# A gated ConvFFN in two stages, its up projection by seven half-size products per pair of column blocks (Strassen's algorithm)

## The chip, the cores and the metric

The kernel runs on one core of one Trainium2 chip. The metric is the device time of one execution in microseconds, as the median of the runs. Engines are named as the profile names them: PE is TensorE's matmul, PEld its weight load, DVE is VectorE, ACT is ScalarE, POOL is GpSimd and SP is the sync engine, whose queue issues most of the DMA transfers.

## The reference

Two trunk layers of a diffusion backbone are computed for 1024 latent tokens and 128 context tokens, 1152 tokens of width 1024 together. Layer 0 mixes with an S5 state-space branch and differential attention, layer 1 with a short convolution and an RG-LRU. Each mixer is followed by a ConvFFN, and every sub-layer stands between two RMSNorms with adaLN modulation. All is float32. The part that matters here:

```python
def conv_ffn(h, w_up, cw, cb, w_down):        # h (1152, 1024), w_up (1024, 5632), w_down (2816, 1024)
    u = dwconv(h @ w_up, cw, 1) + cb          # three taps over the tokens, each sequence by itself
    g, val = jnp.split(u, 2, axis=-1)         # 2816 columns of gate, 2816 of value
    return (jax.nn.gelu(g) * val) @ w_down

def _post(x, y, m, g, j):                     # x + gate * norm(y)
    return x + m[:, 3 * j + 2, None] * rmsnorm(y, g)
```

The modulation m is SiLU(cond) times a matrix of 1024 x 6144 for each layer.

## The kernel before

Matmuls take a rounded float32 type. To keep float32's accuracy each operand is held as two parts, `hi` (a rounded copy, made by ACT) and `lo` (the rest, a subtraction on DVE or POOL), and each product is three matmuls: hi hi, hi lo, lo hi (`mm3`, lines 81 to 87).

The order of the program is: setup and the first norm, S5 with its tables, attention, then `phase_c`: output projection (`mixer_out`), FFN of layer 0 (`ffn`, `down`, `ffn_end`), layer 1's mixer (`mixer1`), its output projection, and the FFN of layer 1. The instructions are written in this order, and a planner (the tile framework) fixes before the run in which order each engine gets them, by a simulated timeline, the order of the program as priority and the free buffers of the pools. On the chip each engine takes its instructions in that order and waits on semaphores.

`mixer_out` (one step for each of 9 token tiles of 128) ends in `pre`, which norms a tile, transposes it on PE, modulates it on ACT, and splits it into `hh` (DVE, line 289) and `hl` (POOL, line 290), the FFN's input as 8 blocks of 128 rows by 1152 tokens.

`ffn` runs over 22 pairs of a gate block and a value block of 128 columns. For each it loads two weight blocks of 512 KB (`wcol`), splits each on ACT (line 97) and DVE (line 99), and for three chunks of 386, 386 and 384 tokens computes both blocks, 24 matmuls each into one PSUM bank (`pps`). ACT scales the middle tap out of PSUM (line 1371), DVE adds the two outer taps, which read the product in PSUM and the sum in SBUF (line 1374), ACT takes the gelu, DVE multiplies gate by value (line 1392), and the result is split into `mh` and `ml` (lines 1393, 1394). Every second pair `down` multiplies the two newest finished pairs by their 128 rows of `w_down`, 9 tiles by 2 halves by 6 matmuls of 512 columns (`dps`), and DVE adds each half to `acc` (line 1420). The `lo` part of `w_down` is made on POOL (line 99). Beside the FFN of layer 0 run 28 pieces of the modulation (`mod_piece`, two per pair at first): 8 loads of 128 KB, 16 DVE instructions on 128x256 (lines 229, 231), a split and four matmuls each. `ffn_end` then does the post norm and the residual tile by tile, and in layer 0 the next pre norm.

`mixer1` makes 20 blocks of 128 columns by `proj`, three chunks of 384 tokens each; its gates are small matmuls of the same chunk width. `tap` (line 1482) is a convolution tap from SBUF to SBUF.

Of the kernel before, what the change touches and what calls it, by code (L numbers as in the profile page):

```python
# [9 lines left out]
F32 = mybir.dt.float32  # L10
# [7 lines left out]
T = 1152  # L18
TS = 1024
# [5 lines left out]
CHF = ((0, 386, 0, 385), (384, 770, 385, 769), (768, 1152, 769, 1152))  # L25


def f(ap):
    return ap.bitcast(F32)

# [23 lines left out]
class K:  # L54
# [59 lines left out]
    # ---------------------------------------------------------------- setup  # L114
    def setup(self):
# [13 lines left out]
        # selector stationaries: column v of ones  # L129
# [17 lines left out]
    # ------------------------------------------------------------ modulation  # L147
# [14 lines left out]
    def finish_row(self, ps, l, j, h0, w, rowp, tag, col=None):  # L162
        """rows of the modulation: + b, and the combination with the norm's gain"""
# [25 lines left out]
    def mod_pe(self, l, js, psp, rowp, tag, cols=None):  # L189
        """rows js of the modulation; a generator, one step for each piece of the weights"""  # L190
# [15 lines left out]
    def mod_cols(self, l, js, pool, ptag, psp, tag, bufs):  # L206
        """rows js of the modulation as columns [128, v, block]"""
# [54 lines left out]
    def post(self, x, y, tmp, ga):  # L262
        """x += gate * norm(y), y in parts"""
        nc = self.nc
        w = D // len(y)
        rs = self.rstd(self.sumsq(y, tmp if self.junk is None else self.junk), D)
        for i, p in enumerate(y):
            sl = slice(i * w, i * w + w)
            nc.vector.tensor_tensor(tmp[:, sl], p, ga[:, sl], op=OP.mult)
        nc.vector.scalar_tensor_tensor(x, tmp, rs, x, op0=OP.mult, op1=OP.add)  # L270

    def pre(self, t, x, tmp, cols, hh, hl):
        """norm of token tile t, transposed, modulated and split into hh, hl"""
# [4 lines left out]
        ts = slice(t * 128, t * 128 + 128)  # L278
        for q in range(2):
            ps = self.pt.tile([128, 4, 128], F32, tag="pt", name=self.nm("tps"))  # L280
            h = self.cv.tile([128, 4, 128], F32, tag="cv", name=self.nm("h"))
# [3 lines left out]
            for i in range(4):  # L285
                b = q * 4 + i
                nc.scalar.activation(h[:, i], ps[:, i], AF.Identity, scale=sc[:, b:b + 1], bias=sh[:, b:b + 1])
            hv = hh[:, q * 4:q * 4 + 4, ts]
            nc.vector.tensor_copy(hv, h)
            nc.gpsimd.tensor_tensor(hl[:, q * 4:q * 4 + 4, ts], h, f(hv), op=OP.subtract)  # L290
# [4 lines left out]
    # ------------------------------------------------------------- projections  # L295
# [46 lines left out]
    def expm1(self, x, one=0.0):  # L342
        """exp(x) - 1 (+ one) of a small array to float32's accuracy"""
# [34 lines left out]
    def unit(self, r, i):  # L378
        """bring a complex number's modulus back to 1"""
# [5 lines left out]
    # ------------------------------------------------------------ S5 parameters  # L385
    def s5_params(self, psp):
# [24 lines left out]
        # angle into [-pi, pi]  # L411
# [24 lines left out]
        # powers a^0 .. a^8  # L436
# [9 lines left out]
        # 10 powers for the read-out side: a^i (forward), a^(9-i) (backward)  # L446
# [5 lines left out]
        # phases e^(i phi) of a^8, and its doublings  # L452
# [7 lines left out]
        # write side: a^(7-j) (forward), a^j (backward), turned back by one chunk  # L460
# [19 lines left out]
        # initial states [ri, d, g, n] -> columns  # L480
# [6 lines left out]
        # first states, the backward scan's turned; one step of the recurrence on them  # L487
# [864 lines left out]
    def ffn(self, l, hh, hl, acc, back):  # L1352
# [4 lines left out]
        for fb in range(NFB):  # L1357
# [46 lines left out]
            if back:  # L1404
                self.mod_piece(*back.pop(0))
# [280 lines left out]
```

## Time and profile before

| what | before |
|---|---|
| median of 3 runs | 3000.33 us (2998.35 to 3001.52) |
| span of the profiled execution, first to last instruction | 2997.2 us |
| busy PE / PEld / DVE / ACT / POOL | 94% / 85% / 68% / 37% / 27% of the span |
| granted TensorE clock, mean | 0.974 of 2.4 GHz |

The profiled execution has no time of its own beside its span; the median of the runs is 3.1 us above it, which is what lies around the span. A busy share says how long an engine had an instruction in hand; an instruction that waits for something while it is in hand counts as busy. Matmuls are pipelined, so one matmul's duration is longer than the distance to the next one; the pace of a stream is its length over its count. In the views by stretch, the columns are the stretch, its length, the busy time and instruction count of PE, PEld, DVE, ACT and POOL, the granted clock, the DMA engines' busy share and GB/s.

### The profile page before, as it was taken

The page shows a single profiled execution, that of the slowest core. Times are in us where ns is not written, and L with a number is a line of the kernel's source. Part 1 is how long each engine was busy: PE and PEld are TensorE (multiplying, and loading weights), DVE is VectorE, ACT ScalarE, POOL GpSimd, SP SyncE. Part 2 cuts the span into 40 slices and gives each one's busy share as a digit, 9 for nine tenths or more (in the row PEclk, how much of TensorE's full clock was granted, in tenths as well). Part 3 has the DMA queues.
Part 4 walks back from the last instruction along what each step waited for, and adds up shares of the span by engine and source line. Part 5 has one row for each costly group of instructions (what it writes and reads, how often), then busy time and mean ns, then how long its engine had stood idle before and what let it go on. Part 6 is the DMA issues. An engine that isn't in the chain of part 4 may idle for free.

```text
span 2997.2 us, 40584 instructions
## 1 busy us (share of the span) xinstructions
PE 2816.8 (94%) x15196; PEld 2557.3 (85%) x15196; DVE 2035.9 (68%) x3572; ACT 1096.7 (37%) x1921; POOL 813.7 (27%) x982
## 2 busy tenths in 40 slices
PE   7976788888999999999999989999999999999998
PEld 3874566777789999999999979997899999999997
DVE  6777765988668888888655685455455555555557
ACT  5222113766454222322222365554532222222222
POOL 2699972877131000000000151112300000000001
PEclk9998899999999999999999999999999999999999
DMA  6434447552642333323211131124411111111113
GB/s 222 142 86 107 117 138 200 137 116 75 193 146 89 98 99 96 97 91 93 62 43 57 64 122 55 53 88 146 138 46 43 43 43 43 43 43 43 43 36 134
DMA packets 298835, 279.45 MB, mean 93 GB/s; under 512 B 45454, under 2 KB 259682, under 8 KB 298638
## 3 DMA queue, kind: packets, MB, share of 16 engines
q1 hardware_dynamic: 266168, 238.51, 25.8%
q0 software_dynamic: 14912, 23.21, 3.1%
q10 hardware_dynamic: 17558, 15.14, 1.8%
q8 instruction: 119, 1.95, 0.3%
q14 instruction: 78, 0.64, 0.1%
HBM read 220.59 MB, written 56.20 MB: 92 GB/s over the span
## 4 chain that ended last, share of the span: by engine, by line
PE 69%; DVE 6%; ACT 3%; issue 2%; DMA 1%; POOL 1%; ACTq 0%; DVEq 0%; POOLq 0%; SPq 0%
PE pps L87 43%; PE dps L87 16%; PE ops L87 6%; DVE e L1077 1%; DVE nb L1060 1%; PE sA L1055 1%; ACT e L1066 1%; PE gps L87 1%; PE tps L284 1%; DVE wh L1102 0%; DVE s L1114 0%; PE ops L1145 0%; DMA mw<-w_mod 0%; POOL hl L290 0%; PE gps L759 0%
## 5 line engine op out<-in xcount | busy, mean ns | idle before, releaser
L87 PE MATMUL pps<-hh,whi 128*128 128x384 f32 (+1 forms) x2880 | 977.0, 339 | 1.1 <-ACT whi L97 0.7
L87 PE MATMUL pps<-hh,wlo 128*128 128x384 f32 (+1 forms) x2880 | 974.7, 339 | 2.2 <-DVE wlo L99 2.2
L87 PE MATMUL pps<-hl,whi 128*128 128x384 f32 (+1 forms) x2880 | 974.7, 339 | 0.6 <-POOL hl L798 0.4
L87 PEld LDWEIGHTS pps<-hh,whi 128*128 128x128 f32 x2880 | 546.1, 190 | 17.5 <-issue 3.2
L87 PEld LDWEIGHTS pps<-hh,wlo 128*128 128x128 f32 x2880 | 545.6, 189 | 15.2 <-DVE wlo L99 3.2
L87 PEld LDWEIGHTS pps<-hl,whi 128*128 128x128 f32 x2880 | 546.4, 190 | 8.1 <-DVE hl L798 0.7
L99 POOL TENSOR_TENSOR wlo<-wr,whi 128x1024 fp32r<-128x1024 f32 x44 | 109.2, 2487 | 1455.3 <-PE dps L87 1162.5
L1374 DVE SCALAR_TENSOR_TENSOR cc<-pps,cvc,cc 128x255 f32<-128x255 f32 (+1 forms) x704 | 342.0, 511 | 145.0 <-ACT cc L1371 139.8
L1420 DVE TENSOR_TENSOR acc<-acc,dps 128x512 f32<-128x512 f32 x360 | 245.9, 683 | 232.5 <-PE dps L87 231.5
L1371 ACT ACTIVATE cc<-pps,cvc 128x383 f32<-128x383 f32 (+2 forms) x264 | 175.0, 665 | 414.1 <-PE pps L87 393.3
L87 PE MATMUL dps<-whi,mh 128*128 128x512 f32 x792 | 311.8, 394 | 1.2 <-DVE acc L1420 1.2
L87 PE MATMUL dps<-whi,ml 128*128 128x512 f32 x792 | 312.0, 394 | 0.0
L87 PE MATMUL dps<-wlo,mh 128*128 128x512 f32 x792 | 310.5, 392 | 0.0
L97 ACT ACTIVATE whi<-wr 128x1024 fp32r<-128x1024 f32 x168 | 177.7, 1059 | 278.3 <-PE pps L87 196.6
L99 DVE TENSOR_TENSOR wlo<-wr,whi 128x1024 fp32r<-128x1024 f32 x124 | 153.9, 1243 | 85.4 <-PE pps L87 70.4
L231 DVE SCALAR_TENSOR_TENSOR macc<-mw,sil,macc 128x256 f32<-128x256 f32 x392 | 174.9, 482 | 18.9 <-DMA mw<-w_mod 18.1
L87 PEld LDWEIGHTS dps<-whi,ml 128*128 128x128 f32 x792 | 148.8, 188 | 33.7
L87 PEld LDWEIGHTS dps<-whi,mh 128*128 128x128 f32 x792 | 149.2, 188 | 20.8 <-DVE acc L1420 2.4
L87 PEld LDWEIGHTS dps<-wlo,mh 128*128 128x128 f32 x792 | 149.2, 188 | 18.8
L1389 ACT ACTIVATE cc<-cc 128x385 f32<-128x385 f32 x132 | 69.3, 525 | 248.1 <-DVE cc L1374 232.2
L1104 POOL TENSOR_TENSOR wl<-wf,wh 128x512 fp32r<-128x512 f32 (+2 forms) x96 | 144.4, 1523 | 52.5 <-DVE ra L1074 44.1
L1394 DVE TENSOR_TENSOR ml<-cc,mh 128x385 fp32r<-128x385 f32 x132 | 118.2, 899 | 34.2 <-ACT mh L1393 34.2
(356 smaller groups left out, 4171.6 us busy)
## 6 DMA issues: line engine op xcount, KB each, us to landing
wr<-ffn_w_up SPq DMA_DIRECT2D x88, 512.0 KB
mw<-w_mod SPq DMA_DIRECT2D x224, 128.0 KB
x<-x SPq DMA_DIRECT2D x45, 512.0 KB
wr<-ffn_w_down SPq DMA_DIRECT2D x44, 512.0 KB
wm<-w_mod SPq DMA_DIRECT2D x40, 512.0 KB
k<-kh POOLq DMA_DIRECT2D x8, 1408.0 KB, 6.4
wr<-w_in_cd SPq DMA_DIRECT2D x20, 512.0 KB
yr<-y SPq DMA_DIRECT2D x17, 512.0 KB
```

Source lines behind the costliest of these rows:

```text
L87: nc.tensor.matmul(ps, x, y, start=first and i == 0 and j == 0, stop=last and i == n - 1 and j == 2)
L97: nc.scalar.activation(hi, raw, AF.Copy)
L99: (eng or nc.vector).tensor_tensor(lo, raw, f(hi), op=OP.subtract)
L231: nc.vector.scalar_tensor_tensor(acc[v], wt, s, acc[v], op0=OP.mult, op1=OP.add)
L284: nc.tensor.transpose(ps[:, i], tmp[:, b * 128:(b + 1) * 128], self.id)
L1055: pin(nc.tensor.matmul(A[:, c:c + w], heads[u.h, 2][:, m, u.q0:u.q0 + 128], heads[u.h, m][:, j, u.k0 + c:u.k0 + c + w], start=j == 0, stop ...
L1104: pin((nc.vector if late else nc.gpsimd).tensor_tensor(vl, u.wf[b][:, :k], f(vh), op=OP.subtract))
L1371: nc.scalar.activation(cc[:, :no], ps[:, q:q + no], AF.Identity, bias=cw[3], scale=cw[1])
L1374: nc.vector.scalar_tensor_tensor(cc[:, oa - o0:ob - o0], ps[:, oa + d - i0:ob + d - i0], cw[j], cc[:, oa - o0:ob - o0], op0=OP.mult, op1=O ...
L1389: nc.scalar.activation(cc[:, :no], cc[:, :no], AF.Gelu_apprx_tanh)
L1394: nc.vector.tensor_tensor(ml[:, o0:o1], g[1][:, :no], f(mh[:, o0:o1]), op=OP.subtract)
L1420: nc.vector.tensor_tensor(acc[t][:, sl], acc[t][:, sl], ps, op=OP.add)
```

## The change

The FFN becomes two stages. `up` writes the rows gelu(g) * val of each pair to DRAM (`m`, 576 KB a pair, by SP); `down` reads them back by token tiles in three groups of 8, 8 and 6 pairs, splits them there, and sums a group's products in two PSUM banks before one addition to `acc`. In the third group each tile's post norm (`ffn_fin`) follows its sum at once.

In `up`, gate and value block form a 2x2 matrix A (rows: gate, value; columns: lower and upper 512 of the inner dimension) and the input a 2x2 matrix B (inner halves by token halves of 576). `forms` builds four combinations T1 to T4 of B's blocks once per layer; `block` builds four combinations of A's blocks per pair on POOL, splits seven half-size weights (four `lo` parts on DVE, three on POOL), makes seven products of 24 matmuls of 288 columns, and adds them up. The convolution then reads the finished rows from SBUF. One piece of the modulation follows each pair in layer 0; the other six go with `down`. The mixer's projections work in two halves of 576 tokens, 48 matmuls of 288 columns each, and PSUM is three double banks and two single ones. The pools become `big` (14 buffers of 9 KB per partition), `mid` (8) and `wr` (8 of 4 KB).

```diff
+    def pair(self, raw, eng, pool=None):
+        p = (pool or self.wr).tile([128, 2] + shape[1:], F32R, tag="big" if pool else "wr", ...)
+        self.nc.scalar.activation(p[:, 0], raw, AF.Copy)
+        eng.tensor_tensor(p[:, 1], raw, f(p[:, 0]), op=OP.subtract)
+    def prod(self, prs, ys, name):
+        ps = self.bank2(name)
+        steps = [(p[:, x, k], y[j][:, k]) for p, y in zip(prs, ys) for k in range(4) for x, j in ((0, 0), (0, 1), (1, 0))]
+        for n, (x, y) in enumerate(steps):
+            for c in range(2):
+                nc.tensor.matmul(ps[:, c, :w], x, y[:, c * w:c * w + w], ...)
+    def forms(self, H):
+        def whole(out, q, n, k, eng):
+            eng.tensor_tensor(out, f(h[:, k]), f(l[:, k]), op=OP.add)
+        def put(i, k, src, eng):
+            nc.scalar.activation(h[:, k], src, AF.Copy)
+            eng.tensor_tensor(l[:, k], src, f(h[:, k]), op=OP.subtract)
+        for k in range(4):
+            whole(A[:, 0], 0, 0, k, G)
+            whole(A[:, 1], 1, 1, k, V)
+            V.tensor_tensor(A[:, 0], r12, A[:, 0], op=OP.subtract)
+            V.tensor_tensor(B[:, 0], A[:, 1], A[:, 0], op=OP.subtract)
+            put(1, k, B[:, 0], G)
+            put(0, k, A[:, 0], V)
+            whole(B[:, 1], 1, 0, k, G)
+            V.tensor_tensor(A[:, 1], A[:, 1], r12, op=OP.subtract)
+            put(2, k, A[:, 1], G)
+            V.tensor_tensor(B[:, 1], B[:, 0], B[:, 1], op=OP.subtract)
+            put(3, k, B[:, 1], V)
+        def block(fb):
+            tt(G, S1, A21, A22, OP.add)
+            tt(G, S2, S1, A11, OP.subtract)
+            A.activation(x, P(A11, B11, V), AF.Copy)
+            tt(G, A21, A11, A21, OP.subtract)
+            p = P(A12, B21, G)
+            tt(V, c11, x, p, OP.add)
+            tt(G, A12, A12, S2, OP.subtract)
+            A.activation(q_, P(A12, B22, V), AF.Copy)
+            yield
+            p = P(S2, T2, G)
+            tt(V, x, x, p, OP.add)
+            A.activation(y, P(S1, T1, V), AF.Copy)
+            tt(G, c12, x, y, OP.add)
+            tt(G, c12, c12, q_, OP.add)
+            p = P(A21, T3, G)
+            tt(V, z, x, p, OP.add)
+            p = P(A22, T4, V)
+            tt(G, c22, z, y, OP.add)
+            tt(V, c21, z, p, OP.subtract)
+            self.up_rest(l, fb, C)
+            if back:
+                self.mod_piece(*back.pop(0))
+            yield
+    def up_rest(self, l, fb, C):
+            nc.scalar.activation(cc, src, AF.Identity, bias=cw[3], scale=cw[1])
+            for j, d in ((0, -1), (2, 1)):
+                for s0, s1 in ((0, TS), (TS, T)):
+                    nc.vector.scalar_tensor_tensor(cc[:, o0:o1], src[:, o0 + d:o1 + d], cw[j], cc[:, o0:o1], ...)
+        nc.vector.tensor_tensor(g[1], g[0], g[1], op=OP.mult)
+        nc.sync.dma_start(self.scratch(f"m{l}", [NFB, 128, T])[fb], g[1])
+    GROUPS = (range(0, 8), range(8, 16), range(16, 22))
+    def down(self, l, finish, back):
+        for gi, fbs in enumerate(self.GROUPS):
+            for fb in fbs:
+                W.append(self.pair(self.load_w(...), nc.gpsimd if fb % 2 else nc.vector, self.big))
+            for t in range(NT):
+                raw = self.wr_tile([128, n, 128], "mr")
+                nc.sync.dma_start(raw, m[fbs[0]:fbs[-1] + 1, :, t * 128:t * 128 + 128].rearrange("f p t -> p f t"))
+                hi, lo = (self.wr_tile([128, n, 128], "m" + x, F32R) for x in "hl")
+                nc.scalar.activation(hi, raw, AF.Copy)
+                nc.vector.tensor_tensor(lo, raw, f(hi), op=OP.subtract)
+                ...
+                    nc.vector.tensor_tensor(acc[t], acc[t], pv, op=OP.add)
+                if gi < 2 and back:
+                    self.mod_piece(*back.pop(0))
+                if gi == 2:
+                    finish(t, acc[t])
...
-            self.proj(self.wcol(w, c0), hh, hl, self.ps, "ps", CH, use)
+            p = self.pair(raw, V, self.big)
+            for n in range(2):
+                use(self.prod([p[:, :, q * 4:q * 4 + 4] for q in range(2)], [H.b[q, n] for q in range(2)], "pps"), ...)
```

## Rows read from the trace of the kernel before

**Rows 1.** The page: its first line, the engines' busy times, the chain by engine.
```profile
span 2997.2 us, 40584 instructions
PE 2816.8 (94%) x15196; PEld 2557.3 (85%) x15196; DVE 2035.9 (68%) x3572; ACT 1096.7 (37%) x1921; POOL 813.7 (27%) x982
...
PE 69%; DVE 6%; ACT 3%; issue 2%; DMA 1%; POOL 1%; ACTq 0%; DVEq 0%; POOLq 0%; SPq 0%
```

**Rows 2.** Busy time by stretch: S5, FFN of layer 0, its end, FFN of layer 1.
```profile
300.00:500.00 200.00, 161.56 (x814) 127.48 (x813) 129.48 (x173) 37.59 (x73) 137.12 (x192) 0.91 0.52 150
...
895.00:1725.00 830.00, 829.04 (x4415) 779.37 (x4414) 644.40 (x1270) 251.65 (x423) 71.11 (x42) 1.00 0.27 82
...
1710.00:1780.00 70.00, 55.74 (x268) 45.92 (x267) 59.21 (x69) 47.58 (x111) 48.16 (x53) 0.90 0.35 125
...
2159.00:2989.00 830.00, 829.77 (x4364) 778.79 (x4362) 473.89 (x747) 233.82 (x363) 68.49 (x46) 1.00 0.17 53
```

**Rows 3.** The chain in order of time (start us, us, what): unbroken runs of matmuls.
```profile
744.37 3.15 PE gps L759 x24
...
1965.90 34.32 PE pps L87 x198
...
2814.26 24.57 PE pps L87 x140
...
2952.01 4.14 PE dps L87 x18
```

**Rows 4.** Line 759, weight loads of the 288-column matmuls: ns min/median/max, first and last start.
```profile
L759 PEld LDWEIGHTS gps<-gg,gw x192: 186/188/338, 744.1 to 783.1; 128*128 128x128 f32 x192
```

**Rows 5.** Timeline of DVE and POOL in the FFN of layer 1 (start us, us).
```profile
2436.57 2.41 POOL L99 TENSOR_TENSOR wlo<-wr,whi 128x1024 fp32r<-128x1024 f32 x1 [69.81 <-PE dps L87]
2437.30 2.09 DVE L1394 TENSOR_TENSOR ml<-cc,mh 128x385 fp32r<-128x385 f32 x1
2439.32 0.67 DVE L1420 TENSOR_TENSOR acc<-acc,dps 128x512 f32<-128x512 f32 x1
2439.92 0.54 DVE L1394 TENSOR_TENSOR ml<-cc,mh 128x384 fp32r<-128x384 f32 x1
2440.15 2.57 POOL L99 TENSOR_TENSOR wlo<-wr,whi 128x1024 fp32r<-128x1024 f32 x1 [1.18 <-ACT whi L97]
2440.38 2.75 DVE L1392 TENSOR_TENSOR cc<-cc,cc 128x383 f32<-128x383 f32 x1
```

**Rows 6.** Timeline of DVE and POOL in the S5 stage, both with work at hand.
```profile
204.10 1.43 POOL L655 TENSOR_TENSOR s<-X,E 128x576 f32<-128x576 f32 x1
205.13 0.42 DVE L916 TENSOR_TENSOR v<-vps,v 128x256 f32<-128x256 f32 x1 [1.61 <-ACT v L915]
205.49 0.62 POOL L531 TENSOR_TENSOR et<-E,Li 128x256 f32<-128x256 f32 x1
205.56 1.16 DVE L657 TENSOR_TENSOR s<-s,s 128x576 f32<-128x576 f32 x1
206.06 1.13 POOL L532 TENSOR_TENSOR et<-E,Lr 128x256 f32<-128x256 f32 x1
206.75 1.05 DVE L656 TENSOR_TENSOR s<-X,E 128x576 f32<-128x576 f32 x1
207.15 1.94 POOL L655 TENSOR_TENSOR s<-X,E 128x576 f32<-128x576 f32 x1
```

**Rows 7.** Single lines by their durations (ns min/median/max), over the whole span.
```profile
L290 POOL TENSOR_TENSOR hl<-h,hh x54: 1257/1294/2260, 815.7 to 2174.3; 128x512 fp32r<-128x512 f32 x54
...
L99 DVE TENSOR_TENSOR wlo<-lwr,whi x4: 681/685/1435, 1776.6 to 1962.2; 128x512 fp32r<-128x512 f32 x4
...
L1485 DVE SCALAR_TENSOR_TENSOR t<-t,lruc,t x16: 342/812/1285, 1826.9 to 2043.1; 128x1023 f32<-128x1023 f32 x8, 128x127 f32<-128x127 f32 x8
```

**Rows 8.** DVE in layer 1's mixer, by line and form (count, busy us, mean ns).
```profile
L1538 DVE TENSOR_TENSOR L<-L 128x1152 f32<-128x1152 f32 x8 | 10.8, 1352 | 0.0
```

**Rows 9.** Timeline of the kernel's end: PE's last matmul.
```profile
2988.38 0.39 PE L87 MATMUL dps<-whi,ml 128*128 128x512 f32 x1
```

More of the change, by code (lines that the diff above doesn't have):

```diff
@@ L24, with two, __init__, raw @@
 CH = ((0, 384), (384, 768), (768, 1152))
-CHF = ((0, 386, 0, 385), (384, 770, 385, 769), (768, 1152, 769, 1152))
+HT = T // 2
 def f(ap):
     return ap.bitcast(F32)
+def two(ap):
+    return ap.rearrange("p (c j) -> p c j", j=HT // 2)
+class Blocks:
+    def __init__(self, k, raws):
+        keys = [(q, n) for q in range(2) for n in range(2) if not (raws and (q, n) == (0, 1))]
+        self.b = {x: [k.big.tile([128, 4, HT], F32R, tag="big", name=k.nm("h" + s)) for s in "hl"] for x in keys}
+        self.r = [k.mid.tile([128, 2, HT], F32, tag="mid", name=k.nm("hr")) for _ in range(2)] if raws else None
+    def raw(self, q, n):
+        return self.r if self.r and (q, n) == (0, 1) else None
+    def parts(self, c0, c1):
+        return [(n, max(c0 - n * HT, 0), min(c1 - n * HT, HT)) for n in range(2) if c0 < n * HT + HT and c1 > n * HT]
 def host_constants():
@@ L1330, in mixer_out @@
                 self.behind(i, self.lastw)
-            yh, yl = (self.mid.tile([128, 8, 128], F32R, tag="mid", name=self.nm(n)) for n in ("yh", "yl"))
+            yh, yl = (self.mid_tile([128, 8, 128], n, F32R) for n in ("yh", "yl"))
             if l == 0:
@@ L1336, in mixer_out @@
                 nc.vector.tensor_tensor(yl[:, s], y, f(yh[:, s]), op=OP.subtract)
-            ps = [self.ps.tile([128, 512], F32, tag="ps", name=self.nm("ops")) for _ in range(2)]
+            ps = self.bank2("ops")
             groups = [[0, 1, 2], [4, 5, 6], [3, 7]] if l and t < 2 else [range(8)]
@@ new lines, in load_w @@
+    def load_w(self, src, shape):
+        raw = self.wr_tile(shape, "wr")
+        i = self.nc.sync.dma_start(raw, src)
+        if self.lastw is not None:
+            self.behind(i, self.lastw)
+            self.lastw = None
+        self.wdma.append(i)
+        return raw
+    def pair(self, raw, eng, pool=None):
+        shape = list(raw.shape)
+        p = (pool or self.wr).tile([128, 2] + shape[1:], F32R, tag="big" if pool else "wr", name=self.nm("wp"))
+        self.nc.scalar.activation(p[:, 0], raw, AF.Copy)
+        eng.tensor_tensor(p[:, 1], raw, f(p[:, 0]), op=OP.subtract)
+        return p
@@ new lines, in up @@
+    def up(self, l, H, back):
+        nc = self.nc
+        V, G, A = nc.vector, nc.gpsimd, nc.scalar
+        w_up = self.a["ffn_w_up"][l]
+        T1, T2, T3, T4 = self.forms(H)
+        B11, B21, B22 = H.b[0, 0], H.b[1, 0], H.b[1, 1]
+        tt = lambda e, o, x, y, op: e.tensor_tensor(o, x, y, op=op)
+        def block(fb):
+            g, v = (self.load_w(w_up[:, b * 128:b * 128 + 128].rearrange("(k p) c -> p k c", p=128), [128, 8, 128]) for b in (fb, NFB + fb))
+            s = self.wr_tile([128, 8, 128], "ws")
+            A11, A12, A21, A22, S1, S2 = (x[:, q:q + 4] for x in (g, v, s) for q in (0, 4))
+            tt(G, S1, A21, A22, OP.add)
+            tt(G, S2, S1, A11, OP.subtract)
+            X = self.mid_tile([128, 2, HT], "X")
+            x, q_ = two(X[:, 0]), two(X[:, 1])
+            C = [self.mid_tile([128, 2, HT], "C")]
+            c11, c12 = (two(C[0][:, n]) for n in range(2))
+            P = lambda raw, B, eng: self.prod([self.pair(raw, eng)], [B], "pps")
+            A.activation(x, P(A11, B11, V), AF.Copy)
[7 more added lines that the diff above has]
+            tt(V, x, x, p, OP.add)
+            Y = self.mid_tile([128, 2, HT], "Y")
+            y, z = two(Y[:, 0]), two(Y[:, 1])
+            A.activation(y, P(S1, T1, V), AF.Copy)
[3 more added lines that the diff above has]
+            tt(V, z, x, p, OP.add)
+            C.append(self.mid_tile([128, 2, HT], "C"))
+            c21, c22 = (two(C[1][:, n]) for n in range(2))
+            p = P(A22, T4, V)
+            tt(G, c22, z, y, OP.add)
+            tt(V, c21, z, p, OP.subtract)
+            self.up_rest(l, fb, C)
@@ L1585, in gate_w @@
         nc, a = self.nc, self.a
-        raw = self.wr.tile([128, 4, 128], F32, tag="wr", name=self.nm("lwr"))
+        raw = self.wr_tile([128, 4, 128], "lwr")
         nc.gpsimd.memset(raw, 0.0)
@@ L1654, in program @@
+            self.down(1, finish1, [])
     def program(self):
```

304 lines of the change are left out of this document (138 added, 166 removed).

## The prediction

> **What bounds the kernel now.** The page comes first: PE is busy for 94% of the span, and the chain that ended last lies for 69% on PE and for 6% on DVE [rows 1]. The views by stretch tell where that holds. The two FFNs take 830 us each, with PE busy throughout and the granted clock at 1.00; DVE is busy for 644 us in layer 0 and 474 us in layer 1, POOL for some 70 [rows 2]. So an FFN lasts as long as its matmuls. The chain in order of time gives their pace [rows 3]: 24.57 us for 140 up matmuls is 0.1755 us each, 4.14 for 18 down matmuls 0.230. An FFN has 22 x 144 = 3168 of the first (556 us) and 22 x 54 = 1188 of the second (273 us): 829 us, the stretch itself. What PE saves there is gained only while no other engine comes to need more than PE.
>
> **PE's work.** A new product of 24 matmuls of 288 columns has its like in S5's gate: 24 in 3.15 us [rows 3]. A weight load of 188 ns stands before each of them [rows 4] and is hidden at a pace of 131 ns, so loading the same weights twice costs nothing. Seven products are 22.05 us per pair, 485 in 22 pairs: 71 us less per layer, **-142**. The mixer's 1440 matmuls at 34.32/198 us [rows 3] become 80 x 24 of 288: 249.6 to 252.0, **+2**. The gates (144 to 192 narrower ones) and the down products do not change.
>
> **What DVE and POOL have to do per pair.** First, how they share. In the FFN of layer 1 a POOL subtraction runs from 2436.57 to 2438.98; a DVE one that needs 0.54 us alone is in hand from 2437.30 to 2439.39, and the next such meeting costs DVE 2.75 us [rows 5]. In S5, POOL and DVE end in turn: 206.11, 206.72, 207.19, 207.80, 209.09 [rows 6]. DVE's 576 elements take 0.61 us after POOL's end, POOL's 576 take 1.29 after DVE's; alone POOL needs 1.43 [rows 6] and DVE about 0.76 (estimate from 0.69 for 512 [rows 7]). They exclude each other. A DVE instruction that reads PSUM is not held up: 0.42 us under a running POOL one [rows 6].
>
> The Trainium skill has this as a rule ("SBUF — State Buffer", section "Who interferes with whom"): a DVE instruction with two inputs in SBUF and a GpSimd one that reads SBUF block each other for the whole instruction. The trace agrees on who is blocked; on the length it shows less, since the start-up of the blocked one is hidden (five instructions end within 3.60 us where their lengths alone sum to 4.2).
>
> Before, this hardly mattered: DVE's taps read PSUM, and POOL had 49 instructions in 830 us [rows 2]. After, a pair gives POOL seven instructions of 512 elements (S1, S2, A21, A12, three lo parts) and three of 576 (c12 twice, c22): 5312 elements. The taps now read SBUF: DVE has 4 x (1023 + 127) elements of taps, a product of 1152 and four lo parts of 512, 7800 elements with two SBUF inputs. Excluding each other by streaming (2.24 and 1.06 ns per element, from 1.29 and 0.61 for 576 [rows 6]) that is 11.9 + 8.3 = **20.2 us** a pair. By lengths alone [rows 7, 8]: POOL 7 x 1.29 + 3 x 1.43 = 13.3, DVE 4 x 0.69 + 4 x (1.28 + 0.34) + 1.35 = 10.6, sum **23.9**. The four additions out of PSUM (0.7 each [rows 5]) are outside.
>
> PE needs 22.05, between the two. In layer 1 I take 22.8: two resources this full, fed in order through eight `wr` buffers, do not run quite without waits. (22.8 - 22.05) x 22 = **+16**; ends 0 and +41.
>
> In layer 0 a piece of the modulation follows each pair. DVE's busy time differs between the FFNs by 644.4 - 473.9 us for 28 pieces [rows 2]: 6.1 us a piece; by streaming alone its 4096 elements with two SBUF inputs take 4.3, with two scalings 4.6. The pair then needs 24.8 to 30.0 us, in either case more than PE. I take 27.0, just on the streaming side, which rows 6 show at work: 4.95 x 22 = **+109**; ends +60 and +175.
>
> By that page of the Trainium skill, taken literally, it would be the upper ends in both layers, +41 and +175.
>
> **The start of `up`.** Before, the first chunk needed only the first tokens. Now `forms` needs the last tile's norm; then POOL runs 16 instructions of 576 (16 x 1.29 = 20.6) and DVE 28 (17.1), excluding each other: 37.7 us. The first halves of pairs 0 and 1 need no forms: 18.9 us of PE work, for which POOL and DVE need 13.6 more. 37.7 + 13.6 - 18.9 = 32. Some of the sums of the first token half can go before the last tile; I take 25 per layer, **+50**; ends 10 and 52 each.
>
> **The third group of `down`.** A tile is 36 matmuls, 8.3 us. Of eight `wr` buffers two tables and one sum hold three; five serve a tile's rows (raw, hi, lo) and the norm's tiles (x, tmp and, in layer 0, h). At the kernel's end, where nothing else runs, the post norm takes 2997.2 - 2988.8 = 8.4 us after the last matmul [rows 1, 9]; layer 0's next norm about doubles it (estimate), and holds three buffers meanwhile. If that serialised fully, 9 x 8 us; if not, nothing. **+20** in layer 0, **+5** in layer 1; ends 0 and 72, 0 and 20.
>
> **Costed at nothing.** The end of layer 0: PE idles 14 us in its 70 us now [rows 2], and the last tile's norms stay exposed; ends -14 and +15. The start of `down`: its first group needs pairs 0 to 7, long written, and buffers that the last pair frees; 3 us per layer, **+6**; ends 0 and 20. The 27 row splits and fewer additions of a layer lie under 273 us of matmuls. `m` out and in: the DMA engines are 17 to 27% busy [rows 2]. But SP takes its queue in order: `m`'s write waits for DVE's product, and behind it stand the next weights and modulation loads. While DVE is ahead this is free; where it is late, the loads are too, which is part of taking 27.0 rather than 24.8.
>
> **Sum**: -142 + 2 + 16 + 109 + 50 + 25 + 6 = +66 us. The span would be 3063 us, and with the 3.1 us around it the median **3066**. The low ends give -74, all high ends +280, which no one run will hold together.
>
> **Rivals.** (A) *Faster.* The planner moves the modulation pieces to where DVE has room (the down groups, 273 us with PE the only full engine), and both layers run at PE's 22.05: -142 + 2 + 50 + 25 + 6 = -59, **2941**. For it: DVE's and POOL's streaming in layer 1 fits, and only pieces in `up` break the fit. Against: the pieces stand in the program behind each pair, and priority follows the program. It wins if a pair of layer 0 takes under some 24 us.
> (B) *Whole lengths count*, start-up and all: 23.9 and 30.0 per pair, and DVE and POOL set both layers: +41 + 175 in place of 125, **3157**. For it: rows 5, where DVE waits out a whole POOL instruction; against: rows 6. (This is what the Trainium skill's page named above says of the block.)
> (C) *The products don't come back to back.* If the planner puts c12's two sums ahead of A21's lo part on POOL, PE waits for 2.9 us of POOL and an eviction of 0.7 in each of 44 pairs: +158, **3224**. A queue simulated for free engines would rather fill POOL with the lo part, which is ready earlier.
>
> PE's clock would not decide it: where PE is busy for about 80% (161.56 of 200 us) the granted clock averages 0.91 [rows 2], and 22.05/0.91 = 24.2 is still under layer 0's 27.0.
>
> **Chances.** The forecast (3010 to 3120) 0.52, A 0.28, B 0.15, C 0.05. About 0.2% (6 us) is what a measurement of this kernel can tell from no change. A lies wholly on the faster side, and a little of the forecast's low end: faster 0.30. Same 0.05. B, C and the rest of the forecast: slower 0.65. The range takes in A with PE's stalls at their small end (about 2915) and B: 2915 to 3165.
>
> **What would show it.** In the views by stretch, the first stage of layer 0's FFN should take about 620 us with PE busy under 90%, and DVE and POOL together over 100% of it; layer 1's about 525. DVE's taps of 1023 should average well over 1.28 us, POOL's 512 over 1.29. PE's waits should name lo parts and sums of POOL and DVE, and 20 to 30 us of them the forms at each start. I am wrong if PE is busy at 98% in layer 0's first stage (A), or if the waits lie at the buffers of the third group instead.

## The result and the profile after

The changed kernel takes 3528.22 us (median of 4 runs, 3525.91 to 3530.92) against 2999.34 us beside it: 1.1765 times as long, 95% interval 1.1748 to 1.1782. The forecast was 3066 with a range to 3165: the direction was right, the size was not.

The page of the kernel after: its first line, the engines' busy times, the granted clock in 40 slices.

```profile
span 3529.1 us, 44056 instructions
...
PE 2848.5 (81%) x16780; PEld 2538.9 (72%) x16780; DVE 2182.9 (62%) x2983; ACT 1225.8 (35%) x1938; POOL 1538.4 (44%) x1428
...
PEclk9989899988889999999997679888988999999987
```

Against [rows 1], PE is no longer the engine that is always busy, POOL has nearly twice the work, and the clock falls in several places. By stretch (columns as in [rows 2]): first the kernel after, in the order mixer_out, up, down, mixer, mixer_out, up, down; then the kernel before: mixer_out, FFN, mixer, mixer_out. Its FFN of layer 1 is in [rows 2].

```profile
790.00:945.00 155.00, 116.51 (x516) 93.76 (x515) 69.64 (x93) 58.85 (x131) 38.05 (x54) 0.87 0.41 128
945.00:1633.00 688.00, 554.39 (x3776) 535.29 (x3776) 662.66 (x801) 245.33 (x348) 406.36 (x237) 0.93 0.29 90
1633.00:2077.00 444.00, 315.96 (x1291) 252.73 (x1291) 168.97 (x239) 107.04 (x184) 64.73 (x65) 0.83 0.27 85
2077.00:2474.00 397.00, 304.35 (x2110) 301.87 (x2111) 157.67 (x213) 144.85 (x156) 35.47 (x17) 0.86 0.15 48
2474.00:2625.00 151.00, 115.70 (x512) 92.60 (x511) 59.36 (x63) 61.50 (x131) 36.34 (x55) 0.88 0.36 115
2625.00:3165.00 540.00, 502.69 (x3696) 500.28 (x3695) 369.27 (x396) 229.26 (x307) 394.11 (x238) 0.96 0.23 75
3165.00:3519.00 354.00, 299.22 (x1188) 238.38 (x1188) 95.64 (x76) 60.81 (x69) 30.04 (x25) 0.89 0.27 83
```

```profile
784.00:895.00 111.00, 108.75 (x503) 89.66 (x504) 66.16 (x99) 52.84 (x123) 32.02 (x46) 0.98 0.46 149
895.00:1764.00 869.00, 855.62 (x4537) 799.92 (x4536) 679.64 (x1309) 280.23 (x489) 102.48 (x75) 0.99 0.27 85
1764.00:2044.00 280.00, 278.73 (x1600) 277.31 (x1600) 156.29 (x228) 156.25 (x207) 42.92 (x24) 0.99 0.23 71
2044.00:2159.00 115.00, 108.91 (x504) 89.22 (x503) 58.64 (x85) 55.41 (x125) 34.99 (x50) 0.99 0.40 139
```

The 532 us between the two profiled spans divide as follows (a stage, down too, begins with its first matmul; the last stage runs to the end of the span):

| stage | before | after | difference | forecast |
|---|---|---|---|---|
| up to mixer_out of layer 0 | 786.3 | 792.0 | +6 | 0 |
| mixer_out, layer 0 | 108.6 | 153.0 | +44 | 0 |
| FFN, layer 0, with the step to the mixer | 869.7 | 688.5 + 443.8 | +263 | +86 |
| mixer, layer 1 | 279.6 | 397.0 | +117 | +2 |
| mixer_out, layer 1 | 114.5 | 150.4 | +36 | 0 |
| FFN, layer 1, to the end | 838.5 | 540.7 + 363.8 | +66 | -22 |

**Layer 0's up is bound by DVE.** It is busy 662.66 of 688 us, PE 554.39. The groups of DVE by line and form (count, busy us, mean ns) in 1105 to 1575, within that stage:

```profile
L254 DVE SCALAR_TENSOR_TENSOR macc<-mw,sil,macc 128x256 f32<-128x256 f32 x220 | 189.3, 909 | 3.8 <-DMA mw<-w_mod 3.6
L1508 DVE SCALAR_TENSOR_TENSOR cc<-C,cvc,cc 128x1023 f32<-128x1023 f32 x61 | 96.2, 1578 | 0.0
L1512 DVE TENSOR_TENSOR cc<-cc,cc 128x1152 f32<-128x1152 f32 x16 | 33.5, 2097 | 0.0
```

The page of the kernel before has the first of these as line 231, with POOL all but idle:

```profile
L231 DVE SCALAR_TENSOR_TENSOR macc<-mw,sil,macc 128x256 f32<-128x256 f32 x392 | 174.9, 482 | 18.9 <-DMA mw<-w_mod 18.1
```

The same instruction takes 909 ns on average instead of 482. There is one product of gate and value (L1512) to a pair; its durations (ns min/median/max), first and last start give the pace, in layer 0 and in layer 1:

```profile
L1512 DVE TENSOR_TENSOR cc<-cc,cc x16: 1337/2438/2447, 1103.9 to 1555.8; 128x1152 f32<-128x1152 f32 x16
...
L1512 DVE TENSOR_TENSOR cc<-cc,cc x17: 1341/1345/1349, 2743.8 to 3103.0; 128x1152 f32<-128x1152 f32 x17
```

Fifteen steps in 451.9 us are 30.1 us a pair, sixteen in 359.2 some 22.4. Layer 1's up, without pieces, is another matter: all of 2730 to 3120 PE is busy at a clock of 1.00. How the two engines hold each other shows in the timeline of layer 0 (without the lines of the other engines):

```profile
1177.46 1.30 POOL L1397 TENSOR_TENSOR wp<-ws,wp 128x512 fp32r<-128x512 f32 x1 [3.20 <-ACT wp L1396]
1177.94 1.36 DVE L1397 TENSOR_TENSOR wp<-ws,wp 128x512 fp32r<-128x512 f32 x1 [0.22 <-ACT wp L1396]
1178.72 1.88 POOL L1448 TENSOR_TENSOR C<-Y 128x576 f32<-128x576 f32 x1
1179.23 3.73 DVE L1508 SCALAR_TENSOR_TENSOR cc<-C,cvc,cc 128x1023 f32<-128x1023 f32 x2
1180.55 2.25 POOL L1397 TENSOR_TENSOR wp<-wr,wp 128x512 fp32r<-128x512 f32 x1
```

DVE's 512 elements end 0.54 us after POOL's instruction (1178.76, 1179.30), POOL's 576 end 1.30 after DVE's (1180.60). An instruction that meets one of the other engine thus waits for its end, and then takes only its streaming time, as in [rows 6]; one that meets none takes its whole length. Of the 220 piece instructions (L254) 105 meet none and take 0.47 us; the other 115 take 1.31 on average.

If the time of each DVE instruction of 1105 to 1575 up to the end of the POOL instruction that it meets is counted as standing, then in these 469 us (some 15.6 pairs) DVE stands behind POOL for 177 us, works for 285 and idles for 7: 11.4, 18.3 and 0.5 us a pair.

**The third group of down is one chain.** The timeline of layer 0, from one tile's last sum to the next one's, without the products' own lines (start us, us):

```profile
1941.41 1.06 ACT L278 ACTIVATE tmp<-acc 128x1024 f32<-128x1024 f32 x1 [11.63 <-issue]
...
1946.07 0.32 SPq L1559 DMA_DIRECT2D x<-acc  x1
...
1946.48 0.39 SPq L1529 DMA_DIRECT2D mr<-m  x1
...
1949.04 1.97 PE L303 MATMUL tps<-misc,tmp 128*128 128x128 f32 x8 [8.97 <-DVE tmp L297]
1950.25 2.90 ACT L310 ACTIVATE h<-tps,mc,mc 128x128 f32<-128x128 f32 x8 [2.97 <-PE tps L303]
...
1953.01 0.88 ACT L1531 ACTIVATE mh<-mr 128x768 fp32r<-128x768 f32 x1
...
1965.43 1.06 ACT L278 ACTIVATE tmp<-acc 128x1024 f32<-128x1024 f32 x1 [11.55 <-issue]
```

The next tile's rows (`mr`) are fetched after this tile's store on SP, and split (L1531) after this tile's modulation on ACT. So norm and products take turns: 24.5 us a tile in layer 0, 15.9 in layer 1, where a tile's 36 matmuls alone take 8.3.

**The mixer** has no engine that is full. What PE waited for in 2077 to 2474 (us, times, longest); in the kernel before no such wait lasted 2 us:

```profile
PE gps L1642 <- ACT L L1643: 60.0, 5, 14.7
PE gps L1642 <- ACT xh L1630: 31.7, 4, 8.1
```

### The profile page after: what moved, and what is told of

It reads as the page before. It is cut to its first block, busy times and chain, and to the rows that moved or that the text cites. A ratio compares the mean times of both kernels' runs of the same rounds, so it can differ in the third digit from the quotient of the medians.

```text
span 3529.1 us, 44056 instructions
## 1 busy us (share of the span) xinstructions
PE 2848.5 (81%) x16780; PEld 2538.9 (72%) x16780; DVE 2182.9 (62%) x2983; ACT 1225.8 (35%) x1938; POOL 1538.4 (44%) x1428
## 5 line engine op out<-in xcount | busy, mean ns | idle before, releaser
L1408 PE MATMUL pps<-hh,wp 128*128 128x288 f32 x3392 | 631.6, 308 | 67.7 <-ACT wp L1396 44.0
L1408 PEld LDWEIGHTS pps<-hh,wp 128*128 128x128 f32 x3392 | 532.1, 200 | 73.1 <-ACT wp L1396 45.6
L1537 PE MATMUL dps<-wp,mh 128*128 128x512 f32 x1584 | 460.3, 412 | 90.6 <-ACT mh L1531 90.6
L1537 PEld LDWEIGHTS dps<-wp,mh 128*128 128x128 f32 x1584 | 315.1, 201 | 165.7 <-ACT mh L1531 98.3
L1397 POOL TENSOR_TENSOR wp<-wr,wp 128x512 fp32r<-128x512 f32 (+1 forms) x110 | 225.0, 2048 | 411.0 <-ACT wp L1396 404.7
L1408 PE MATMUL pps<-hl,wp 128*128 128x288 f32 x1696 | 382.5, 307 | 0.0
L1508 DVE SCALAR_TENSOR_TENSOR cc<-C,cvc,cc 128x1023 f32<-128x1023 f32 (+1 forms) x352 | 360.6, 1064 | 20.0 <-ACT cc L1504 20.0
L254 DVE SCALAR_TENSOR_TENSOR macc<-mw,sil,macc 128x256 f32<-128x256 f32 x392 | 298.5, 807 | 18.3 <-DMA mw<-w_mod 17.6
L1396 ACT ACTIVATE wp<-wr 128x512 fp32r<-128x512 f32 (+1 forms) x284 | 198.9, 723 | 306.4 <-POOL wr L1448 131.7
L1408 PEld LDWEIGHTS pps<-hl,wp 128*128 128x128 f32 x1696 | 291.1, 200 | 0.0
L1537 PE MATMUL dps<-wp,ml 128*128 128x512 f32 x792 | 262.8, 414 | 22.9 <-DVE ml L1532 22.8
```

The costliest lines, as they stand in the source:

```text
L254: nc.vector.scalar_tensor_tensor(acc[v], wt, s, acc[v], op0=OP.mult, op1=OP.add)
L1396: self.nc.scalar.activation(p[:, 0], raw, AF.Copy)
L1397: eng.tensor_tensor(p[:, 1], raw, f(p[:, 0]), op=OP.subtract)
L1408: nc.tensor.matmul(ps[:, c, :w], x, y[:, c * w:c * w + w], start=n == 0, stop=n == len(steps) - 1)
L1508: nc.vector.scalar_tensor_tensor(cc[:, o0:o1], src[:, o0 + d:o1 + d], cw[j], cc[:, o0:o1], op0=OP.mult, op1=OP.add)
L1537: nc.tensor.matmul(ps[:, h], x[:, i], W[i][:, y, h * 512:h * 512 + 512], start=i == 0 and j == 0, stop=i == n - 1 and j == 2)
```

## The experiments

Each was run on the chip; times without an interval are of one run and one profile, the kernel before beside them at 2998.55 to 3002.14. Theory: Strassen's products cost what POOL and DVE take from each other in layer 0, and the starts; everything else lost is order and room in the stages around them.

**Pieces moved to down.**

```diff
-                self.up(0, H, back)
+                self.up(0, H, [])
...
-                if gi < 2 and back:
-                    self.mod_piece(*back.pop(0))
+                for _ in range(2 if gi == 0 or t < 5 else 1):
+                    if gi < 2 and back:
+                        self.mod_piece(*back.pop(0))
```

> All 28 modulation pieces of layer 0 move from the up stage to the first two groups of down (two per tile, then one). Theory: in layer 0 DVE is full (462.7 of 470 us) because the pieces meet POOL's instructions; without them its up stage is bound by PE like layer 1's, 688 us falls to 540 to 560, and down (444 us with the transition) grows by 60 to 130, since DVE then needs more than the 11 us of a tile; the whole 10 to 90 us faster. Rival: the sums and lo parts alone hold layer 0's up stage (its products wait for them in any case): it stays above 630 us.

3518.31 us. Layer 0's up falls from 688.5 to 542.9, layer 1's length (539.7); down with the step grows from 443.8 to 584.9, 11 us over the expected 60 to 130. The stage behaves as the theory says, but the work has no free place: 146 us won, 141 given back; the whole, 10 us, is at the low end of what was expected.

**Without the weight sums.**

```diff
-            s = self.wr_tile([128, 8, 128], "ws")
-            A11, A12, A21, A22, S1, S2 = (x[:, q:q + 4] for x in (g, v, s) for q in (0, 4))
-            tt(G, S1, A21, A22, OP.add)
-            tt(G, S2, S1, A11, OP.subtract)
+            A11, A12, A21, A22, S1, S2 = (x[:, q:q + 4] for x in (g, v, v) for q in (0, 4))
...
-            tt(G, A21, A11, A21, OP.subtract)
...
-            tt(G, A12, A12, S2, OP.subtract)
```

> Left out: the four sums of weight blocks that POOL makes for each pair (S1, S2, and the new A21 and A12); the products take the loaded blocks instead, as many of them and as long. DVE's work is untouched. Theory (DVE and POOL hold each other up for whole instructions): a pair of layer 0 loses some 4 x 1.3 us of exclusion, 29.7 us falls to 24 to 26, the stage by 80 to 125 us; the 256-column instructions of the pieces, 909 ns on average now, fall to 650 to 800. Layer 1's pair stays at 22 (PE). Rival (DVE's own instructions fill it, POOL's don't matter): layer 0's stage moves by under 25 us.

3412.63 us. Layer 0's up takes 596.7 (92 less), with DVE's instructions as many as before. DVE by line and form in 1000 to 1470:

```profile
L254 DVE SCALAR_TENSOR_TENSOR macc<-mw,sil,macc 128x256 f32<-128x256 f32 x248 | 174.3, 741 | 1.6 <-DMA mw<-w_mod 1.5
```

Taking work from POOL makes DVE's instructions shorter: 741 ns for 909. A pair now takes 25.4 us, 4.7 less; the four sums, at the 1.15 us that each of them takes after a DVE instruction's end, would be 4.6. (The edit also frees one of the eight `wr` buffers and spares four products the wait for a sum, which no run sets apart.) Layer 1's up loses 17 us (523.2), at its start; once it runs, PE is busy all the time (360 of 360 us in 2640 to 3000 here, 390 of 390 in 2730 to 3120 before the edit), so that a pair can't gain.

**All of POOL's share on DVE.** The test from the other side.

```diff
-        V, G, A = nc.vector, nc.gpsimd, nc.scalar
+        V, G, A = nc.vector, nc.vector, nc.scalar
...
-        V, G = nc.vector, nc.gpsimd
+        V, G = nc.vector, nc.vector
```

> All of POOL's work in the up stages and the forms goes to DVE: four sums of weights, three lo parts, three sums of products per pair, 16 instructions per start. DVE then has, by lengths without exclusion, 4 taps 6.5, the product 1.35, seven lo parts 4.8, four weight sums 2.8, three output sums 2.3, four sums out of PSUM 3.0: 20.7 us a pair, and some 5 to 6 for a modulation piece. Theory (POOL's work costs DVE as much as it takes off it, or more): layer 0's pair falls from 29.7 to 26 to 27.5 us, its stage by 45 to 80 us; layer 1's pair stays at 22 to 22.8. Rival (DVE's own load is the limit and POOL relieves it): layer 0's pair rises to 36 us or so, its stage by over 100 us.

3386.96 us, 141 less. Up of layer 0 and of layer 1 by stretch, and DVE by line and form in 1040 to 1500:

```profile
945.00:1470.00 525.00, 505.30 (x3740) 503.92 (x3740) 511.16 (x838) 232.38 (x331) 8.89 (x4) 0.97 0.31 97
2498.00:3017.00 519.00, 501.88 (x3696) 500.48 (x3696) 443.71 (x631) 231.94 (x309) 9.74 (x5) 0.97 0.25 77
```

```profile
L1508 DVE SCALAR_TENSOR_TENSOR cc<-C,cvc,cc 128x1023 f32<-128x1023 f32 x80 | 103.6, 1295 | 0.6 <-ACT cc L1504 0.6
L254 DVE SCALAR_TENSOR_TENSOR macc<-mw,sil,macc 128x256 f32<-128x256 f32 x146 | 65.9, 468 | 2.3 <-DMA mw<-w_mod 2.3
L1397 DVE TENSOR_TENSOR wp<-wr,wp 128x512 fp32r<-128x512 f32 x93 | 62.6, 674 | 0.0
```

Both layers are now at PE's pace, and layer 1's start is 21 us shorter (540.7 to 519.3). It went further than expected in layer 0 (688.5 to 524.8): the planner let about half of the pieces slip into down (11 stay in up, 21 did before), which takes 40 us more (484.0). So up's 164 us are not POOL's alone; the 141 us of the whole kernel are net of what down gave back. The rival (DVE's own load is the limit and POOL relieves it) falls. In layer 0 DVE does POOL's ten instructions of a pair in 7 x 0.67 + 3 x 0.74 = 7 us; leaving them on POOL cost DVE 14 x (909 - 468) ns on the pieces, 4 x (1578 - 1295) on the long taps, and 0.65 on the product: 8 us on these lines alone. In layer 1, with no pieces, a pair takes 22.4 us either way, and only the start gains.

**Plain products in the same two stages.**

```diff
+            for b in (fb, NFB + fb):
+                raw = self.load_w(...)
+                p = self.pair(raw, self.nc.vector, self.big)
+                C.append(self.mid_tile([128, 2, HT], "C"))
+                for n in range(2):
+                    ps = self.prod([p[:, :, q * 4:q * 4 + 4] for q in range(2)], [H.b[q, n] for q in range(2)], "pps")
+                    self.nc.scalar.activation(two(C[-1][:, n]), ps, AF.Copy)
+            self.up_rest(l, fb, C)
...
-            H = Blocks(self, True)
+            H = Blocks(self, False)
```

> The two stages, the pools, down and the mixers stay; only Strassen's part goes: each half of a block is two ordinary products (8 of 24 matmuls a pair instead of 7), no combinations, no forms, POOL idle in up, and the input's eight tiles all in big, so that mid has two more free buffers. Theory (what up lost in layer 0 is DVE against POOL, and what it lost at each start are the forms): 22 x 8 x 3.15 = 554 us in either layer, plus up to 10 at the start, so layer 0 688 to 555 to 575, layer 1 541 to 555 to 565; the whole 95 to 130 us faster. Rival (the stage as such, taps from SBUF and pieces on DVE, is the limit in layer 0): its up stage stays above 620 us. Beside it: if the two tiles of H in mid make the hole after tile 4 of mixer_out, that stage falls from 150 to 120 to 130; if it is the loads' order on SP, it stays.

3401.91 us, 126 less. Both up stages by stretch:

```profile
936.00:1505.00 569.00, 568.95 (x4303) 568.95 (x4304) 374.12 (x657) 204.50 (x249) 12.90 (x5) 1.00 0.36 110
2475.00:3041.00 566.00, 565.74 (x4224) 565.74 (x4225) 223.47 (x243) 186.53 (x206) 11.04 (x5) 0.99 0.23 72
```

As the theory said: in this kernel Strassen's part costs layer 0's up 119 us (688.5 for 569.3) and saves 25 in layer 1 (540.7 for 565.8). The stage as such is not the limit; even with all pieces in it, layer 0's up stays at PE's pace.

mixer_out's matmuls (first to last) also shorten, from 133 to 113 us and from 133 to 110. In layer 0 the first five row loads go out by 815.2 in both kernels; the sixth in the kernel after, and in this one:

```profile
867.33 0.78 SPq L1356 DMA_DIRECT2D yr<-y  x1
```

```profile
822.87 0.46 SPq L1356 DMA_DIRECT2D yr<-y  x1
```

With two more free buffers in `mid`, the hole is gone (in 860 to 880 PE was busy for 5.67 us of 20 in the kernel after). The stage keeps only part of it, 140 us instead of 150 in layer 1, since 30 us pass from its last matmul to up's first, not 17. The run changes `big` and the products as well, so it points to `mid` and does not prove it.

**Buffers or order in the third group.** Three runs: two buffers of their own for x and tmp; the same with the next tile's rows ahead; and that order alone.

```diff
+                if self.xw is None:
+                    self.mpx.close()
+                    self.xw = P("xw", 2)
...
-        x = self.wr_tile([128, D], "x")
...
-        tmp = self.wr_tile([128, D], "tmp")
+        x, tmp = (self.xw.tile([128, D], F32, tag="xw", name=self.nm(n)) for n in ("x", "tmp"))
```

```diff
             for t in range(NT):
+                hi, lo = nxt or rows(t)
...
                 if gi == 2:
+                    if t + 1 < NT:
+                        nxt = rows(t + 1)
                     finish(t, acc[t])
```

> Two buffers of 4 KB of their own, in the room that the modulation's pools leave free before the third group, for x and tmp of the FFN's post norm in both layers, and for x in layer 1's mixer_out; the other eight stay. Theory (the eight wr buffers tie tile t + 1's rows to tile t's norm): the third group falls from 24.3 to 12 to 16 us a tile in layer 0 and from 15.9 to 9 to 11 in layer 1, 75 to 110 and 45 to 60 us, and layer 1's mixer_out from 150 to 120 to 130 because the rows' loads no longer stand behind a load of x that waits for a buffer; the whole 140 to 200 us faster. Rival (the chain of a tile's norm through ACT, POOL, DVE and PE in their fixed order is what takes the time, buffers or not): third group within 20 us of now in either layer.

> The buffers of the run before (two of their own for x and tmp), and in the third group the next tile's rows are loaded and split ahead of this tile's norm in the order of the program. Theory (in layer 0 the order is what serialises: the next rows' load stands behind this tile's store on SP, their split behind this tile's eight modulations on ACT): a tile of layer 0 falls from 24 to 10 to 14 us, the group by 90 to 125 us, the whole to 3350 to 3385; layer 1 as in the run before (9 to 10 us). Rival (the norm's chain itself takes over 20 us a tile in layer 0): within 25 us of the run before.

> The same order alone, with the eight wr buffers as they were. Theory (order decides in layer 0, buffers in layer 1): layer 0's third group falls as with both, to 10 to 16 us a tile; layer 1's stays near 16. Rival (both are needed in both layers: five buffers can't hold two tiles' rows beside x, tmp and h): layer 0 stays above 20 us a tile.

3473.44, 3389.84 and 3389.17 us. Last eight tiles of the third group by stretch, layer 0 and layer 1: first with buffers alone, then with order alone. The columns here are the stretch, its length, PE's busy time and count on down's products (`dps`) alone, the granted clock, the DMA share and GB/s.

```profile
1872.00:2067.00 195.00, 83.56 (x288) 0.71 0.19 60
3397.00:3463.00 66.00, 64.54 (x285) 1.00 0.45 164
```

```profile
1868.00:1984.00 116.00, 82.02 (x288) 0.85 0.32 101
3313.00:3378.00 65.00, 64.04 (x283) 1.00 0.51 172
```

In layer 1 either cure brings 8.2 us a tile, PE's pace (my theory that only buffers would was wrong). In layer 0 buffers do nothing (24.5 us a tile), order brings 14.4, and both together bring no more. Down wins 77 us in layer 0 (with the step to the mixer) and 61 in layer 1 from the order alone. In layer 1's mixer_out own buffers for x changed nothing (150.4), against the theory: its row loads came as late as before.

**The mixer.** Gates in their own banks; then also the next x ahead, with mixer_out's loads ahead of the norm before.

```diff
-                        ps = self.bank2("gps")[:, :, :HT // 2]
+                        for c in range(2):
+                            o = n * HT + c * (HT // 2)
+                            ps = self.pt.tile([128, 512], F32, tag="pt", name=self.nm("gps"))[:, :HT // 2]
```

```diff
+        lru_x(0)
         for j in range(4):
             lru_branch(j)
+            if j < 3:
+                lru_x(j + 1)
             conv_branch(j)
```

> The gates' products of layer 1's mixer go to the two single PSUM banks, a quarter (288 tokens) at a time, so that they no longer share three double banks with the projections. Nothing else moves. Theory: the second direction's gates fill all three banks while their sigmoids wait for the first direction's scan (PE waits 60 us for L1643), and the projections that could run have no bank: the mixer's 397 us fall to 290 to 320, the whole by 75 to 110. Rival: the big pool's 14 buffers (8 input, 3 scan, 3 for weights) hold the projections back: the mixer moves by under 25 us.

> Gates in their own banks as before; and in layer 1's mixer the next scan branch's first projection (x) goes ahead of the convolution branch's three in the order of the program. In mixer_out, next tile's loads and splits go ahead of this tile's norm. Theory: PE's 8 us wait for the convolution of x before each branch's gates (31.6 us in four) gets the convolution branch's products as cover, and the clock, 0.89 now, returns to 1.00 with it: the mixer falls from 359 to 285 to 315. Rival (the buffers for weights, or DVE and ACT, hold it): over 340. For mixer_out: theory (order) 150 to 120 to 130 in layer 1 and 25 us less in layer 0; rival (mid's six free buffers): within 10 us of now.

3490.99 and 3445.28 us; the mixer takes 359.3 and 327.2. PE's waits, of the first run and of the second:

```profile
PE gps L1642 <- ACT xh L1630: 31.6, 4, 7.9
PE pps L1408 <- ACT wp L1396: 14.0, 4, 4.0
PE gps L1642 <- ACT L L1643: 3.8, 3, 3.0
```

```profile
PE pps L1414 <- ACT wp L1402: 14.0, 4, 4.0
PE gps L1654 <- ACT xh L1642: 7.9, 1, 7.9
```

Each edit removes the wait that it was aimed at, 60 us to 4 and 32 to 8, and the stage falls by 38 and by 32 more. Both were expected to bring more (290 to 320, 285 to 315): when the gates' wait goes, a wait for split weights grows from 2 us to 14, and the granted clock in the stage is 0.86 in the kernel after and still 0.83 to 0.98 in the second run. 48 us over the kernel before stay open. In mixer_out, loads ahead gave 10 us in layer 1 and 3 in layer 0.

**All together**, first with plain products, then with Strassen's (POOL's share on DVE), then with more room and order in mixer_out and the third group.

```diff
-        ga = [self.table(self.wr, "wr", l, 2, v) for v in range(2)]
+        ga = [self.table(self.wr, "wr", l, 2, 0)]
...
+                        fetch(t + 2)
...
+                if t > 2:
+                    self.behind(i, stores[t - 3])
```

> The two stages with plain products (the run without Strassen's part, 3402 us), with the rows ahead in the third group, the gates in their own banks and the projection of x ahead, mixer_out as that run has it. Theory (the losses lie in separate stages and add): 3402 - 77 - 61 - 66 = 3198, between 3180 and 3220; still 6% or so over the kernel before, since two mixer_out, two group changes of down and half of the mixer's loss stay. Rival (they hide behind one another): over 3230.

> Strassen's products with all that the runs alone showed: POOL's share of up on DVE, rows ahead in the third group, gates in their own banks, the projection of x ahead, mixer_out's loads ahead. Theory (the stages add): 3387 - 77 - 61 - 70 - 10 = 3169, between 3150 and 3195: below the plain products with the same mending (3197), since up takes 525 and 519 us here against 569 and 565 there, and down takes up to 40 us more in layer 0 with the pieces that up no longer has room for. Rival (the pieces and the mended third group want DVE at the same time): 3200 or more.

> The same, and in mixer_out and the third group: the gate table of the context tile only loaded for that tile (a wr buffer free until then), x and tmp of the post norm in two buffers of their own, the rows loaded two tiles ahead, and a y load ordered behind the store of three tiles before on SP, so that loads don't fill mid. Theory: layer 0's third group, 15 us a tile with its rows' load behind the store before, falls to 10 to 12 (30 to 45 us), mixer_out by 10 to 20 in each layer: 3085 to 3140. Rival (the norm's chain on ACT and DVE, 13 us of ACT and 10 of DVE a tile, holds it where it is): 3150 or more. Neither expects it below the kernel before.

3197.0 us (1.0652 of before, interval 1.0634 to 1.0670), 3164.64, and 3168.83 (1.0562, 1.0544 to 1.0579). The first two came within 5 us of the sums: the losses lie in separate stages and add. The third brought nothing: it ends where its rival said (3150 or more), but not for the load that the rival gave. In layer 0's third group most tiles still take 14 to 18 us, and ACT is busy for 6 us of one and DVE for 7, so neither is full; that the norm's chain of waits holds them is argued, not tried. In both Strassen versions one tile takes far longer, 36 us in the second and 45 in the third: the last two pieces of the modulation have slipped into the third group, and PE waits for them there (of the third version):

```profile
PE mps L261 <- ACT mhi L258: 16.8, 2, 9.4
```

Up, down, up, down of the second, by stretch:

```profile
938.00:1464.00 526.00, 505.27 (x3740) 503.90 (x3740) 512.26 (x836) 231.65 (x330) 10.93 (x4) 0.97 0.31 96
1464.00:1873.00 409.00, 318.02 (x1327) 255.55 (x1327) 248.63 (x437) 113.59 (x202) 59.49 (x63) 0.86 0.39 119
...
2339.00:2857.00 518.00, 499.23 (x3696) 497.95 (x3696) 444.22 (x631) 233.25 (x310) 10.52 (x5) 0.98 0.25 77
2857.00:3153.00 296.00, 275.33 (x1188) 226.01 (x1188) 96.66 (x78) 60.56 (x68) 27.20 (x24) 0.95 0.32 101
```

From its first up matmul (2339.3) to its end (3162.9), layer 1's FFN takes 823.6 us against 838.5 before: there Strassen's algorithm does win, 15 us of the 71 that PE saves. Layer 0's FFN is still 66 over, the mixer 48, layer 1's mixer_out 24, and all up to layer 0's first up matmul 43: together the 166 us by which the span is longer. None of the versions beats the kernel before.

## Why the prediction failed

The sum missed 466 us of the span, by stage: 177 in layer 0's FFN, 115 in the mixer, 88 in layer 1's FFN, 80 in the two mixer_out and 6 ahead of them. What PE saves was right; what failed are the steps that priced the stages around it.

- **PE's products, -71 a layer**: right. A pair takes 22.4 us, for the 22.05 of the sum, wherever nothing else holds PE.
- **Layer 1's pair, 22.8**: right within its bounds. Its start, "I take 25", was too low: up took 540.7 us, 56 over 485, of which the pairs are 8, so the start costs nearer to the end of 52. Without POOL it is some 27. Layer 1's up missed by 15 us in all.
- **Layer 0's pair, "I take 27.0, just on the streaming side, which rows 6 show at work"**: too low, 30.1. The exclusion itself came as [rows 6] show it: POOL held DVE up for 11.4 us a pair, where the sum has 11.9. What failed is DVE's own work, 8.3 + 4.6 in the sum by streaming and 18.3 in the trace. Most of its instructions meet none of POOL's and take their whole length (0.47 us for 256 elements, 0.27 by streaming), and the four additions out of PSUM (0.74 each), which the sum sets outside, fill the same engine. Rival B's 30.0 came near by luck: it counts POOL's instructions whole and leaves those additions out, and its 23.9 for layer 1 did not show. With the start, up missed by 69 us (688.5 for 619). The Trainium skill calls the port that the two engines share an exclusive lock ("SBUF — State Buffer", section "Who interferes with whom"); the trace agrees, 0.54 us from POOL's end to DVE's. Beside it "Perfetto Trace Analysis" of the Trainium skill, section "Optimizing Scalar/DVE Operations", says that moving work between DVE and GpSimd might not help; the run without POOL shows more, 141 us gained by not moving it.
- **The third group, +20 and +5**: of the terms in my sum the one that missed most. Over 8.3 us a tile it cost 130 and 61 us; the order alone wins 77 and 61 of that. It had the place and an end of 72, but sought the cause in free buffers. What I missed is that the program puts a tile's norm ahead of the next tile's rows, and that SP and ACT keep that order: a load behind a store, a split behind eight modulations.
- **The mixer, "+2"**: I counted matmuls and called it done, though the change also put projections and gates into the same three double banks. +117: 38 by the banks, 32 by the order, 48 not settled.
- **mixer_out**: not in my sum at all. +44 and +36. Its matmuls, first to last, take 25 and 20 us more; late row loads make that hole, and the run with two more buffers in `mid` is without it. From the last of them to up's first product pass 20 and 17 us, for 0.6 in the kernel before: the last tile's norm stands before that product on PE, and PE waits 9.5 us for it in layer 0. No run tried that part alone.
- **PE's clock "would not decide it"**: no run sets its share apart, but idle stretches brought it down where I had none: 0.73 in layer 0's third group, 0.86 in the mixer.
- **Group changes of down**: not costed. Layer 1's last tile of the first group is summed up at 3267.6 and the next at 3296.9, 18 us more than the 10.9 of a tile; layer 0's takes 19 more. The change to the third group costs nothing (8.2 us to its first sum).
- **Slips in the working**: the high ends add up to +307, not +280, and [rows 2] have 42 and 46 POOL instructions, not 49. Neither changes the forecast, and +529 lies above all the high ends together.
- **Rival A** (2941) asked for layer 0 at PE's pace; the run without POOL gives just that, 524.8 us, and still ends at 3387, for all that A left at its small end lies elsewhere.

## What to carry to other kernels

When an edit changes pools, banks and the order of stages along with its arithmetic, cost every stage that shares them, not only the one that it is named after: 364 of the 529 us here came back with the products as they are (3528.22 to 3164.64). Work moved from DVE to POOL is not free work: if both read SBUF, and DVE two inputs of it, price each POOL instruction as time in which DVE stands (1.15 us for 512 elements here), beside all of DVE's own instructions at their whole length, and compare that with DVE doing it itself (0.67). And where a loop ends each step in a long dependent tail, put the next step's loads and splits ahead of that tail in the program: here the queues kept the order that the program gave.

## What the runs showed of the hardware

In layer 0 POOL as a helper was worth less than nothing: DVE does ten POOL instructions in 7 us a pair, and stood 11 us a pair behind them when POOL had them. A meeting costs a DVE instruction 1.0 to 1.2 us whatever its own length (medians: 127 columns went from 0.34 to 1.36 us, 256 from 0.47 to 1.51, 1023 from 1.27 to 2.45), so short instructions lose most for their size. An addition with one input in PSUM is not held: 0.74 us with POOL running and without.

And gaps cost PE more than their length: in the eight tiles of 24.5 us with buffers alone, half of each idle, the granted clock was 0.71 and PE was busy for 84 us with the 288 matmuls; layer 1's eight tiles without gaps had 1.00 and 65 us. In the kernel after, one tile's first four matmuls, behind two waits of 9 and 3 us with eight transposes between them, start 0.50 us apart at a granted clock of 0.50 (the 1.2 GHz level, 2052.98 to 2054.99); six later ones 0.23 apart at 1.00 (2.4 GHz, 2057.03 to 2058.41).
